# Sixteen of 31 taps of a depthwise convolution as 32x32 diagonal products on the tensor engine

## The chip, the cores and the metric

The kernel runs on one core of a Trainium2 chip, as one program with one launch. The metric is the time of one execution in device microseconds. The engines are TensorE (PE in the profile), VectorE (DVE), ScalarE (ACT), GpSimd (POOL) and SyncE (SP), which issues DMAs.

## The reference, cut to what matters

The program is a small network in float32; the change concerns the convolution inside its "even mixer". That mixer projects 512 latent tokens and 256 context tokens with one matrix. The first columns of the result are gated and go through a depthwise convolution of 31 taps along the tokens, each of the 512 channels with its own 31 weights, and then a layer norm and a SiLU. The rest are queries, keys and values of an attention.

```python
def depthwise_conv(x, w, b=None):
    width = w.shape[0]
    left = (width - 1) // 2
    y = lax.conv_general_dilated(x, w[:, None, :].astype(x.dtype), (1,), [(left, width - 1 - left)],
                                 dimension_numbers=('NWC', 'WIO', 'NWC'), feature_group_count=x.shape[-1])
    return y if b is None else y + b
...
def conformer_conv(p_glu, conv_w, conv_b, ln_g, ln_b):
    a, gate = jnp.split(p_glu, 2, axis=-1)
    u = depthwise_conv(a * jax.nn.sigmoid(gate), conv_w, conv_b)
    return jax.nn.silu(layer_norm(u, ln_g, ln_b))
...
def even_mixer(...):
    p_lat = h_lat @ w_in
    conv_lat = conformer_conv(p_lat[..., :EV_Q0], conv_w, conv_b, ln_g, ln_b)
    q_lat = apply_axial_rope(qk_heads(p_lat[..., EV_Q0:EV_K0]), rope)
    k_lat = apply_axial_rope(qk_heads(p_lat[..., EV_K0:EV_V0]), rope)
    v_lat = v_heads(p_lat[..., EV_V0:])
    ...
```

## The kernel before

Activations lie with features on the 128 partitions and tokens along the free axis. The 512 channels of the convolution are four tiles `conv[0]` to `conv[3]`, and each has two regions of tokens, 512 latent and 256 context columns. A scheduler fixes one static order of instructions for each engine before the run; a loop's generator steps only suggest which work is near which.

Dense products are float32 in three products of two float32r parts. `wsplit` loads a weight piece with a DMA (`wraw`, three buffers), ACT rounds it to `whi` (L73), and VectorE, or GpSimd for four of the tiles, subtracts to get `wlo` (L74), two buffers each. `gemm` then issues L90, L91 and L92 for each of eight row tiles.

The even mixer has three stretches here. In the first part (about 80 to 218 us) the eight gating projections run together with the filter spectra of another layer (the `hy...` names). VectorE forms the gated inputs `us` (whose tile has the name `xl`, L420) and tap 0 of the convolution (L421). In the q/k stage (about 218 to 309) eight tiles of queries and keys are projected, 512 and then 256 columns each. VectorE applies the rotary embedding (L494 to L496) and GpSimd adds its two terms (L497). In the v stage (about 309 to 375) the value projection follows (columns of 256, evacuated by ACT at L511) and the layer norm of the convolution `conv_norm` (its mean's products at L465, its broadcast at L121). Then attention begins (`S`, L571). Between the weight tiles, steps of modulation products are inserted (`mods`, L153): they use the four column strips of the array, 32 output partitions each, and L157 copies their bank on ACT.

The remaining 30 taps are written as a generator, one step per channel tile and region. Taps 29 and 30 are products on ACT and sums on GpSimd (L444, L447, L448, L452); taps 1 to 28 are 28 multiply-adds on VectorE, one after another on the same output (L449 to L451):

```python
for j in range(1, 29):
    nc.vector.scalar_tensor_tensor(out=o, in0=u[:, j:j + n], scalar=cw[:, i, j:j + 1], in1=o,
                                   op0=ALU.mult, op1=ALU.add)
nc.gpsimd.tensor_tensor(out=o, in0=o, in1=o2, op=ALU.add)
```

The scheduler has moved many of the taps forward into the first part, as soon as a tile's inputs exist. PSUM has eight banks of 512 float32 columns. In the even mixer four are the main pool `ps`, two belong to the modulation products (`mps`), and two to the filter spectra in the first part and to the norm (`cps`) afterwards.

`sum4` is a constant of 128 rows by 32 columns, four 32x32 identities above one another. A product with it as the stationary operand adds four groups of 32 partitions.

## Time and profile before

| what | value |
|---|---|
| time, median of 3 runs | 3722.39 us (3717.83 to 3723.65) |
| span of the profiled execution | 3715.1 us |
| TensorE, VectorE busy in the span | 3512.9 us, 2178.3 us |
| ACT, GpSimd busy in the span | 1375.5 us, 740.5 us |
| mean granted TensorE clock | 0.979 of full speed |

The profiled execution is known by its span, from its first instruction to its last; beside it stand the three timed runs, whose median is 7.3 us longer. Busy time of TensorE includes time in which a product runs at a lower clock. A granted clock of 1 is the level of 2.4 GHz.

### The profile page before, as it was taken

How to read it: one execution, taken by the hardware profiler on the slowest of the kernel's cores; microseconds unless marked ns; L12 is line 12 of the kernel's file. 1: busy time of each engine (PE TensorE's matmuls, PEld its weight loads, DVE VectorE, ACT ScalarE, POOL GpSimd, SP SyncE). 2: the span in 40 equal slices, each digit the busy share in tenths (PEclk: the TensorE clock that was granted, in tenths of full speed). 3: DMA queues.
4: the chain of work that ended last, by engine and by line, in shares of the span. 5: the costliest groups of instructions: out<-in, count | busy, mean ns of one | idle time of the engine just before them, and what ended most of it. 6: DMA issues, size and time to landing. Idle time of an engine off the chain costs nothing.

```text
span 3715.1 us, 52350 instructions
## 1 busy us (share of the span) xinstructions
PE 3512.9 (95%) x20932; PEld 2830.7 (76%) x20932; DVE 2178.3 (59%) x3655; ACT 1375.5 (37%) x2393; POOL 740.5 (20%) x637
## 2 busy tenths in 40 slices
PE   6998989999998899989999989999999989999999
PEld 4766778888887667667888877768888877778887
DVE  7998876544458765554333676654334676754333
ACT  4213643222226434233223444542223554642222
POOL 0133201102203333211111032022112132013111
PEclk9998999999999999999999999999999999999999
DMA  5244113333323223332222313233333213243232
GB/s 197 80 159 131 49 50 124 122 119 119 118 102 116 84 75 101 99 130 79 97 92 96 111 55 105 91 127 94 94 96 103 98 52 121 71 133 92 91 96 91
DMA packets 146172, 376.99 MB, mean 101 GB/s; under 512 B 18023, under 2 KB 42983, under 8 KB 145544
## 3 DMA queue, kind: packets, MB, share of 16 engines
q1 hardware_dynamic: 145928, 373.65, 31.0%
q8 instruction: 164, 2.69, 0.3%
q14 instruction: 80, 0.66, 0.1%
HBM read 341.61 MB, written 28.84 MB: 100 GB/s over the span
## 4 chain that ended last, share of the span: by engine, by line
PE 54%; DVE 7%; ACT 3%; issue 2%; POOL 2%; DMA 0%; SPq 0%; DVEq 0%; POOLq 0%; ACTq 0%
PE acc L90 16%; PE acc L92 16%; PE acc L91 16%; DVE wlo L74 1%; DVE hb L1576 1%; PE rec L1301 1%; PE rec L1302 1%; PE rec L1286 1%; ACT whi L73 1%; ACT mp L1811 0%; DVE oz L819 0%; PE acc L1378 0%; PE acc L1377 0%; PE acc L1379 0%; POOL yt L1542 0%
## 5 line engine op out<-in xcount | busy, mean ns | idle before, releaser
L73 ACT CAST whi<-wraw 128x1024 fp32r<-128x1024 f32 (+2 forms) x508 | 493.9, 973 | 1353.4 <-PE acc L91 1014.1
L74 DVE TENSOR_TENSOR wlo<-wraw,whi 128x1024 fp32r<-128x1024 f32 (+2 forms) x504 | 584.2, 1160 | 204.5 <-ACT whi L73 198.0
L90 PE MATMUL acc<-hh,whi 128*128 128x512 f32 (+1 forms) x1024 | 368.2, 360 | 10.9 <-ACT whi L73 7.7
L92 PE MATMUL acc<-hh,wlo 128*128 128x512 f32 (+1 forms) x1024 | 365.3, 358 | 10.2 <-POOL wlo L74 5.6
L91 PE MATMUL acc<-hl,whi 128*128 128x512 f32 (+1 forms) x1024 | 366.5, 358 | 0.7 <-DVE hl L256 0.3
L90 PE MATMUL acc<-fhh,whi 128*128 128x512 f32 x704 | 279.4, 397 | 0.0
L91 PE MATMUL acc<-fhl,whi 128*128 128x512 f32 x704 | 279.1, 396 | 0.0
L92 PE MATMUL acc<-fhh,wlo 128*128 128x512 f32 x704 | 279.1, 396 | 0.0
L91 PE MATMUL acc<-hidl,whi 128*128 128x512 f32 (+1 forms) x768 | 274.4, 357 | 0.9 <-DVE hidl L85 0.9
L90 PE MATMUL acc<-hidh,whi 128*128 128x512 f32 (+1 forms) x768 | 274.6, 358 | 0.0
L92 PE MATMUL acc<-hidh,wlo 128*128 128x512 f32 (+1 forms) x768 | 274.3, 357 | 0.0
L341 POOL TENSOR_TENSOR sqr<-relu 128x512 f32<-128x512 f32 (+1 forms) x96 | 130.6, 1362 | 682.6 <-ACT relu L339 682.6
L90 PEld LDWEIGHTS acc<-hh,whi 128*128 128x128 f32 x1024 | 196.1, 192 | 51.1 <-ACT whi L73 12.5
L92 PEld LDWEIGHTS acc<-hh,wlo 128*128 128x128 f32 x1024 | 195.5, 191 | 43.8 <-DVE wlo L74 7.5
L91 PEld LDWEIGHTS acc<-hl,whi 128*128 128x128 f32 x1024 | 197.2, 193 | 32.8 <-DVE hl L256 2.7
L92 PE MATMUL acc<-shh,wlo 128*128 128x512 f32 (+1 forms) x480 | 194.1, 405 | 8.2 <-DVE wlo L74 8.2
L90 PE MATMUL acc<-shh,whi 128*128 128x512 f32 (+1 forms) x480 | 195.7, 408 | 3.5 <-ACT whi L73 3.5
L91 PE MATMUL acc<-shl,whi 128*128 128x512 f32 (+1 forms) x480 | 194.7, 406 | 0.0
L91 PEld LDWEIGHTS acc<-hidl,whi 128*128 128x128 f32 x768 | 145.3, 189 | 24.5 <-DVE hidl L85 1.3
L90 PEld LDWEIGHTS acc<-hidh,whi 128*128 128x128 f32 x768 | 144.3, 188 | 23.3
L92 PEld LDWEIGHTS acc<-hidh,wlo 128*128 128x128 f32 x768 | 144.3, 188 | 22.9
L92 PEld LDWEIGHTS acc<-fhh,wlo 128*128 128x128 f32 x704 | 132.6, 188 | 32.3
(630 smaller groups left out, 7912.9 us busy)
## 6 DMA issues: line engine op xcount, KB each, us to landing
wraw<-in_mlp_w_dram SPq DMA_DIRECT2D x128, 512.0 KB, 3.2
wraw<-in_ada_w_dram SPq DMA_DIRECT2D x96, 512.0 KB, 3.8
wraw<-in_w_in_dram SPq DMA_DIRECT2D x58, 512.0 KB, 3.3
wraw<-in_w_gate_dram SPq DMA_DIRECT2D x44, 512.0 KB, 3.5
wraw<-in_w_up_dram SPq DMA_DIRECT2D x44, 512.0 KB, 3.5
wraw<-in_od_w_fm_dram SPq DMA_DIRECT2D x36, 512.0 KB, 3.3
wraw<-in_w_down_dram SPq DMA_DIRECT2D x32, 448.0 KB, 3.3
wraw<-in_hy_dft_dram SPq DMA_DIRECT2D x34, 256.0 KB, 2.6
```

Of the source, the lines that this page charges most:

```text
L73: nc.scalar.copy(hi, raw)
L74: (eng or nc.vector).tensor_tensor(out=lo, in0=raw, in1=f32(hi), op=ALU.subtract)
L90: nc.tensor.matmul(out, s[0], m[0], start=first, stop=False)
L91: nc.tensor.matmul(out, s[0], m[1], start=False, stop=False)
L92: nc.tensor.matmul(out, s[1], m[0], start=False, stop=last)
L341: nc.gpsimd.tensor_tensor(out=s, in0=r, in1=r, op=ALU.mult)
L1286: nc.tensor.matmul(vn_ps[pf[d], hd], wT[:, c, pf[d]], S[:, c], start=True, stop=True)
L1301: nc.tensor.matmul(op_[pf[d], hd], qd[:, c, pf[d]], S[:, c], start=True, stop=False)
L1302: nc.tensor.matmul(op_[pf[d], hd], at[pf[d], c], vn[pf[d], hd], start=False, stop=True)
L1576: nc.vector.tensor_tensor_scan(out=b[:, hd], data0=rst, data1=lf[:, hd], initial=0.0, op0=ALU.mult, op1=ALU.add)
```

## The change

Taps 13 to 28, sixteen of them, leave VectorE. For each channel tile and region (a unit) `strips` makes 64 products on TensorE. The stationary operand of one is a 32x32 block with one tap's 32 weights on its diagonal (`dia`, made once by four GpSimd products), and the moving one is 32 channels of the gated input, shifted by the tap. The row strip `q` of the array is the group of 32 channels and chooses one of four PSUM banks; the column strip `s` is one of four taps and chooses 32 output partitions of the bank. Four rounds cover the 16 taps and accumulate. ACT copies the four banks to `e` (tile `cve`). One unit later `joined` adds the four taps' parts with `sum4`, one product per group of channels; ACT copies the result (`cv4`) and VectorE adds it to `conv`.

The PSUM pools change: `ps` has three banks instead of four; the modulation products have two banks only in the block that comes before the first part, and one afterwards; `cps` has four from the q/k stage on.

```diff
+P0, PT = 13, 16
...
-        ps = hp.enter_context(k.pool("evps", 4, space=PSUM))
-        mps = hp.enter_context(k.pool("evmps", 2, space=PSUM))
+        ps = hp.enter_context(k.pool("evps", 3, space=PSUM))
...
-                with k.pool("ada", side="right") as mp:
+                with k.pool("ada", side="right") as mp, k.pool("evmps", 2, space=PSUM) as mps:
...
+        mps = hp.enter_context(k.pool("evmps1", 1, space=PSUM))
+        cps = hp.enter_context(k.pool("evcps", 4, space=PSUM))
...
+            dia = pp.tile([128, 4, PT, 32], F32, name="cdia")
+            for i in range(4):
+                nc.gpsimd.tensor_tensor(out=dia[:, i], in0=k.sum4.unsqueeze(1).to_broadcast([128, PT, 32]),
+                                        in1=cw[:, i, P0:P0 + PT].unsqueeze(2).to_broadcast([128, PT, 32]), op=ALU.mult)
+
+            def strips(i, r):
+                c0, n = regs[r]
+                bank = [k.tmp([128, 512], "acc", pool=cps, bufs=None) for _ in range(4)]
+                for t in range(0, PT, 4):
+                    for s in range(4):
+                        for q in range(4):
+                            p = slice(32 * q, 32 * q + 32)
+                            u0 = c0 + 30 * r + P0 + t + s
+                            nc.tensor.matmul(bank[q][32 * s:32 * s + 32, :n], dia[p, i, t + s], us[p, i, u0:u0 + n], start=t == 0, stop=t + 4 >= PT)
+                e = k.tmp([128, 4, T], "cve", bufs=1, pool=pp)
+                for q in range(4):
+                    nc.scalar.copy(e[:, q, :n], bank[q][:, :n])
+                return i, r, e
+
+            def joined(i, r, e):
+                c0, n = regs[r]
+                acc = k.tmp([128, 512], "acc", pool=ps, bufs=None)[:, :n]
+                for q in range(4):
+                    nc.tensor.matmul(acc[32 * q:32 * q + 32], k.sum4, e[:, q, :n], start=True, stop=True)
+                o3 = k.tmp([128, T], "cv4", bufs=1, pool=pp)[:, :n]
+                nc.scalar.copy(o3, acc)
+                o = conv[i][:, c0:c0 + n]
+                nc.vector.tensor_tensor(out=o, in0=o, in1=o3, op=ALU.add)
...
             def taps():
+                last = None
                 for i in range(4):
                     for r, (c0, n) in enumerate(regs):
+                        new = strips(i, r)
+                        if last:
+                            joined(*last)
+                        last = new
...
-                        for j in range(1, 29):
+                        for j in range(1, P0):
...
+                joined(*last)
                 for r in range(2):
                     yield from conv_norm(r)
...
-            cps = hp.enter_context(k.pool("evcps", 2, space=PSUM))
```

The static order shows where the products stand. In the changed kernel the lines have other numbers: the gemm's three products are L92 to L94, the modulation products L155 and L162, the strips L456, the joining products L467, the mean of the norm L508 and its broadcast L123. Buffer numbers follow the names.

On TensorE, before, the end of one q/k tile (256 columns), a modulation step and the start of the next tile (512 columns):

```order
L92 MATMUL acc_1765<-hh,wlo_1731 128x256
L153 MATMUL acc_1614<-wraw_1825,cs 32x512 x2
L153 MATMUL acc_1614<-wraw_1829,cs 32x512 x2
L90 MATMUL acc_1839<-hh,whi_1835 128x512
L91 MATMUL acc_1839<-hl,whi_1835 128x512
L92 MATMUL acc_1839<-hh,wlo_1836 128x512
```

At the same boundary in the change, the last of a unit's 64 strip products (context region) stands ahead, then the joining products of the unit before it:

```order
L456 MATMUL acc_1860<-xl_505,cdia 32x256
L467 MATMUL acc_1930<-cve_1763,sum_90 32x512 x4
L155 MATMUL acc_1623<-wraw_1956,cs 32x512 x2
L155 MATMUL acc_1623<-wraw_1960,cs 32x512 x2
L92 MATMUL acc_1970<-hh,whi_1966 128x512
L93 MATMUL acc_1970<-hl,whi_1966 128x512
L94 MATMUL acc_1970<-hh,wlo_1967 128x512
```

One whole unit stands between two tiles of the q/k stage, in one piece.

On VectorE, before, in the q/k stage, one tile's rotary embedding and the `wlo` of the next weight, with taps behind it (the two kinds alternate for 16 rows until the next embedding):

```order
L494 STREAM_SHUFFLE rt_364_1760<-acc_1734 128x512
L495 TENSOR_TENSOR rt_363_1759<-acc_1734,c_rope2d 128x512
L496 TENSOR_TENSOR rt_364_1760<-rt_364_1760,c_rope2d 128x512
L74 TENSOR_TENSOR wlo_1836<-wraw_1833,whi_1835 128x1024
L450 SCALAR_TENSOR_TENSOR conv_113<-xl_504,c_ev_conv_w,conv_113 128x256
L450 SCALAR_TENSOR_TENSOR conv_114<-xl_504,c_ev_conv_w,conv_114 128x512
```

At the next tiles of the change, the add of a joined unit (L471) stands where the taps were:

```order
L76 TENSOR_TENSOR wlo_1967<-wraw_1964,whi_1966 128x1024
L471 TENSOR_TENSOR conv_109<-conv_109,cv_377_1935 128x512
L536 STREAM_SHUFFLE rt_387_1996<-acc_1970 128x512
L537 TENSOR_TENSOR rt_386_1995<-acc_1970,c_rope2d 128x512
L538 TENSOR_TENSOR rt_387_1996<-rt_387_1996,c_rope2d 128x512
L76 TENSOR_TENSOR wlo_2137<-wraw_2134,whi_2136 128x1024
L471 TENSOR_TENSOR conv_109<-conv_109,cv_395_2105 128x256
```

From here on VectorE has no tap left in the q/k stage; all remaining ones stand ahead.

On TensorE, before, the mean's products of the norm (L465) stand among the v products:

```order
L92 MATMUL acc_2547<-whi_2475,hl 128x256
L90 MATMUL acc_2547<-whi_2491,hh 128x256
L465 MATMUL acc_2577<-ones,cv_451_2573 128x1 x4
L90 MATMUL acc_2612<-whi_2475,hh 128x256
L91 MATMUL acc_2612<-wlo_2476,hh 128x256
```

In the change they stand close behind the joining products of the last latent unit, with two modulation steps between, and the broadcast (L123) follows at once:

```order
L456 MATMUL acc_2886<-xl_505,cdia 32x256
L467 MATMUL acc_2956<-cve_2781,sum_90 32x512 x4
L155 MATMUL acc_2305<-wraw_2982,cs 32x512 x2
L162 MATMUL acc_2988<-c_ada_sel,wraw_2986 128x4 x4
L508 MATMUL acc_3106<-ones,cv_507_3102 128x1 x4
L123 MATMUL acc_3113<-diag_3114,ones 128x128
```

So the norm's first products now come directly behind the last strips and ahead of most of the v products.

## Rows read from the trace of the kernel before

**Rows 1.** The page's head: the span, then each engine's busy time, share and instructions.
```profile
span 3715.1 us, 52350 instructions
...
PE 3512.9 (95%) x20932; PEld 2830.7 (76%) x20932; DVE 2178.3 (59%) x3655; ACT 1375.5 (37%) x2393; POOL 740.5 (20%) x637
```

**Rows 2.** Windows by stage, one core: length, busy us of each engine, clock, DMA share, GB/s.
```profile
80.00:218.00 138.00, 122.39 (x555) 93.21 (x553) 129.50 (x196) 41.36 (x66) 26.80 (x16) 0.95 0.31 100
218.00:309.00 91.00, 81.96 (x456) 62.74 (x456) 90.72 (x141) 15.54 (x25) 37.80 (x19) 0.98 0.40 138
309.00:375.00 66.00, 53.56 (x377) 45.23 (x377) 48.47 (x80) 24.89 (x43) 21.16 (x15) 0.87 0.49 150
```

**Rows 3.** Waits of TensorE, 80 to 218, eight kinds: us in total, times, longest.
```profile
PE acc L92 <- DVE wlo L74: 5.1, 6, 1.4
...
PE acc L90 <- DVE hyspec L713: 0.2, 1, 0.2
```

**Rows 4.** The same view, 218 to 375.2, nine kinds.
```profile
PE acc L90 <- ACT whi L73: 6.7, 4, 5.3
PE acc L92 <- POOL wlo L74: 5.6, 3, 2.4
PE acc L91 <- DVE wlo L74: 3.4, 2, 2.4
PE acc L92 <- DVE wlo L74: 2.2, 3, 1.0
```

**Rows 5.** Timeline of TensorE, 228 to 239: start, us, line, tiles, shapes.
```profile
228.37 0.50 PE L90 MATMUL acc<-hh,whi 128*128 128x512 f32 x1
...
230.13 0.40 PE L90 MATMUL acc<-hh,whi 128*128 128x512 f32 x1
230.37 0.39 PE L91 MATMUL acc<-hl,whi 128*128 128x512 f32 x1
...
237.25 1.06 PE L153 MATMUL acc<-wraw,cs 128*32 128x512 f32 x8
238.25 0.50 PE L90 MATMUL acc<-hh,whi 128*128 128x512 f32 x1
238.59 0.40 PE L91 MATMUL acc<-hl,whi 128*128 128x512 f32 x1
```

**Rows 6.** Groups of VectorE by line and form, 66 to 400: busy, mean ns.
```profile
L450 DVE SCALAR_TENSOR_TENSOR conv<-xl,c_ev_conv_w,conv 128x512 f32<-128x512 f32 x112 | 96.7, 864 | 0.0
L450 DVE SCALAR_TENSOR_TENSOR conv<-xl,c_ev_conv_w,conv 128x256 f32<-128x256 f32 x112 | 66.9, 597 | 0.1
```

**Rows 7.** Records of line L153, 237.20 to 237.60, then to 238.20: ns min/median/max, first and last start.
```profile
L153 PE MATMUL acc<-wraw,cs x4: 617/617/617, 237.3 to 237.3; 128*32 128x512 f32 x4
...
L153 PE MATMUL acc<-wraw,cs x8: 592/604/617, 237.3 to 237.7; 128*32 128x512 f32 x8
```

**Rows 8.** Timeline of TensorE, 1229.8 to 1231.
```profile
1229.86 0.75 PE L1201 MATMUL prep<-R,LM 32*32 32x32 f32 x64
```

**Rows 9.** Groups of ACT by form, 66 to 400.
```profile
L511 ACT COPY vv<-acc 128x256 f32<-128x256 f32 x12 | 4.4, 369 | 16.0 <-PE acc L92 16.0
...
L157 ACT COPY wraw<-acc 128x512 f32<-128x512 f32 x3 | 1.8, 587 | 2.0 <-PE acc L153 1.7 <-issue 0.4
```

**Rows 10.** Groups of VectorE by form, 66 to 400.
```profile
L471 DVE TENSOR_TENSOR conv<-conv,acc 128x512 f32<-128x512 f32 x4 | 2.7, 680 | 0.0
```

**Rows 11.** Groups of GpSimd by form, 66 to 400.
```profile
L452 POOL TENSOR_TENSOR conv<-conv,cv 128x512 f32<-128x512 f32 x4 | 7.6, 1910 | 36.8 <-DVE conv L450 36.8
```

**Rows 12.** Timeline of all engines, 308 to 322.
```profile
309.76 5.32 DVE L450 SCALAR_TENSOR_TENSOR conv<-xl,c_ev_conv_w,conv 128x512 f32<-128x512 f32 x8
...
311.66 0.83 ACT L554 CAST QS<-b 64x768 fp32r<-64x768 f32 x1 [2.93 <-POOL b L497]
...
314.45 0.58 PE L90 MATMUL acc<-whi,hh 128*128 128x256 f32 x1 [5.34 <-ACT whi L73]
```

**Rows 13.** Windows, 310 to 320.
```profile
310.00:320.00 10.00, 3.15 (x12) 1.20 (x13) 10.00 (x12) 6.66 (x8) 6.78 (x4) 0.56 0.20 61
```

## The prediction

> **What bounds the kernel now.** I read the page first. TensorE is busy for 95% of the span and VectorE for 59% [rows 1], so a change that moves work from VectorE to TensorE must find a stretch in which VectorE, not TensorE, sets the pace. The windows of the even mixer are such a candidate: VectorE is busy 129.5 of 138 us in its first part and 90.7 of 91 us in the q/k stage [rows 2]. But TensorE is not idle there either: 122.4 of 138, 82.0 of 91 and 53.6 of 66 us. What TensorE leaves idle in the three windows is 15.6 + 9.0 + 12.4 = 37 us, and no relief of VectorE can return more than that, apart from the clock.
>
> The waits of TensorE say what the idle time is. Its eight kinds in the first part run from 5.1 us on the `wlo` pieces of VectorE down to 0.2 and add up to 14.7 us [rows 3]. The nine kinds in the q/k and v stages add up to 22.3 us: 6.7 on the ACT cast `whi`, 5.6 on the GpSimd `wlo`, 3.4 + 2.2 on the VectorE `wlo`, and the rest on five others [rows 4]. The timeline shows what a q/k tile costs when nothing is late: 9.88 us from one tile's first product (228.37) to the next one's (238.25), in a stretch without a wait: 24 products of 512 columns at 0.23 to 0.24 us, 24 of 256 at half of that, and the block of modulation products [rows 5]. Eight tiles took 91 us, 11.4 each. So TensorE's own work is 87% of a tile there, and VectorE's fullness costs about 1.5 us a tile.
>
> The longest single wait shows how VectorE's taps reach TensorE [rows 12]. Eight taps stand together from 309.76 for 5.32 us; the rope results that ACT casts to `QS` come late (311.66, after 2.93 us idle for GpSimd's sum), the weight cast `whi` stands behind such casts, and TensorE starts its v product at 314.45 after 5.34 us. In 310 to 320 the granted clock is 0.56, a mean that lies between the levels 1.2 and 2.4 GHz and close to the lower one [rows 13].
>
> **The change, part by part.** *Taken from VectorE:* 128 of the 224 taps, 64 of 512 columns at 864 ns and 64 of 256 at 597 [rows 6]: 55.3 + 38.2 = 93.5 us of VectorE. Eight adds replace them, at most 8 x 0.68 = 5.4 us [rows 10]. VectorE has 269 us of work in 295; after it about 181. It is then not the limit of any of the three windows.
>
> *Added to TensorE:* 512 products of 32 rows by 32 columns, 64 for each of eight units (four channel tiles times a stream of 512 and one of 256 tokens). The trace has no such product with a long moving side. The nearest rows are the modulation products: also float32, 512 columns, on the four column strips. Four of them show eight records, so each product takes two passes: four records start at 237.3 (617 ns each), and four more by 237.7 [rows 7]. The four strips run beside one another, and a pass lasts about 0.45 us (the block of 8 occupies 1.00 us to the next tile's start, which with two passes is at most 0.50; twice a 512-column product's 0.234 is 0.47; the starts lie 0.4 apart). That row strips also run beside one another is shown by 64 records of 32x32 products on diagonal tiles that take 0.75 us together, 12 ns each [rows 8]. So I take all 16 tiles of the array as running together. A unit then has four rounds (16 taps over four column strips) of two passes: 8 x 0.45 = 3.6 us for 512 columns and 1.8 for 256. Entering and leaving such a block costs some 0.3 us (237.25 to 238.25 is 1.00 for two passes of 0.45; the product before it ends its slot 0.09 earlier, and the tile's second product follows at 0.34 instead of 0.23) [rows 5]. Four channel tiles: 4 x (3.9 + 2.1) = 24.0 us. The joining products are four column strips once, two passes, 0.9 and 0.45 us: 4 x 1.35 = 5.4 us. **TensorE gets 29.4 us more.** None of it is hidden: TensorE runs its queue in order, and its only empty slots are the waits counted below.
>
> The lower end, with passes of 0.40 us, is 26.6 us. The upper ends come from how far the 16 tiles hold one another up, and are the rivals below.
>
> The Trainium skill (TensorE: Matmul & The Clock Gate, Part 3, "The mechanism") says that matmuls start and end strictly in program order. Taken literally, a product's second pass waits for its own first pass, and everything behind it too; [rows 7], with four first passes at 237.3 and the second ones at 237.7, speak against so strict a reading. By that rule the sum would be the last rival's.
>
> *Given back, q/k and v stages.* Of the 22.3 us of waits, those on the `whi` casts (6.7) and on the VectorE `wlo` pieces (5.6) stand behind taps and should go: **-12.3**. The GpSimd `wlo` (5.6) stays: GpSimd keeps its sums and gets four products of 128x512 (about 4 x 1.9 = 7.6 us by its nearest row) [rows 11]. The 4.4 us of others stay.
>
> *Given back, first part.* In VectorE's order, 55 taps of 512 and 37 of 256 columns stand ahead of the first part's last evacuation before, and 42 and 36 after. That is 13 x 0.864 + 0.6 = 11.8 us less. TensorE waits 14.7 us there, mostly for VectorE's pieces. A share of one half, **-6**, lies between nothing (the weights are late for other reasons, and the main PSUM pool drops from four banks to three) and the whole 11.8.
>
> *Given back, clock.* The window 309 to 375 runs at 0.87 [rows 2], which costs it (1 - 0.87) x 66 = 8.6 us against full speed. Denser work there may hold the clock: I take half, **-4**.
>
> *Hidden.* ACT makes 32 + 8 copies of banks: 20 x 0.587 + 20 x 0.369 = 19.1 us [rows 9]; it is busy 40 of 157 us in the last two windows, and a unit's copies (2.3 us) have a whole tile of about 14 us until its four banks are wanted again. If that cover is gone, each is on TensorE's way with 2.3 us. The modulation products lose one of two banks; their copy and transposition (0.6 us, three times) are small.
>
> *New waits.* In TensorE's order the norm's products (L508) stand right behind the joining products of the last unit of 512 columns, with two steps of modulation between. Joining leads to them by an ACT copy (0.59), the add into `conv` (0.68) and the last add of the mean's sum (0.68 by the same row): 1.9 us in which TensorE has one modulation block, and behind it stand the norm's broadcast and the `v` products, which attention waits for. I put **+2**, since the broadcast's own small steps follow as well. The four copies of the unit ahead (2.3 us) lie beside the unit of 256 columns (2.1) that TensorE runs in between.
>
> *Sum.* 29.4 - 12.3 - 6 - 4 + 2 = +9.1 us on the profiled 3715.1. The median of the three runs, 3722.4, is 7.3 above the span, so 3722.4 + 9.1 = 3731.5: **3732 us**. A change within 0.2% (7.4 us) can hardly be told from none; the forecast stands just above that edge.
>
> **The rivals.**
> 1. *Forecast,* the 16 tiles together with the returns as put down: 3732, own range 3717 to 3742. Chance 0.43.
> 2. *VectorE is the true pace of the first part and the q/k stage (faster).* Then every us taken from it ahead of the last evacuation returns (11.8), all waits of the later stages go (22.3), and the clock comes back in full (8.6): 29.4 - 42.7 = -13.3, 3709 (the 2 us at the norm are then covered too). For it: 99.7% busy in 218 to 309. Against it: 9.88 of 11.4 us of a tile are TensorE's own. It decides for faster once more than 37 us come back. Chance 0.20.
> 3. *New waits take the recovery's place.* The chain at the norm lies bare from the four copies on (2.3 + 0.9 + 1.9 with the same again for the broadcast, some 7 in place of 2) and three banks cancel the first part's 6: +20, 3742. Against it: VectorE empties banks sooner. Chance 0.18.
> 4. *Second passes block a strip.* The four products of one tap can run together, but the next tap's wait for a pass: 16 slots of 0.45 us a unit, 7.2 and 3.6, so 4 x 11.4 (with edges) + 5.4 = 51; the returns stay at 22.3 and the norm's 2: +31, 3753. Chance 0.12.
> 5. *Only four tiles ever run together:* 16 rounds of two passes, 14.4 and 7.2: 4 x 22.2 + 5.4 = 94, net +74, 3796. Chance 0.05.
> 6. *Each product waits for its own first pass:* 64 x 0.45 = 28.8 us for a unit of 512, 14.4 for one of 256: 4 x 43.8 + 5.4 = 181, net +160, 3883. The strict order of the Trainium skill's page would give this. Chance 0.02.
>
> **How the numbers follow.** The range runs from 3708 (the faster rival) to 3756 (the fourth); about 0.07 lies above, some 0.1 below. Faster than 3715: 0.15 of rival 2, 0.03 of the forecast's spread: 0.18. Within 0.2%: 0.05 of rival 2, 0.17 of the forecast, 0.04 of rival 3: 0.26. Slower than 3730: the rest, 0.56.
>
> **What would show it.** In the rows of the diagonal products (L456, 1,024 records): a block of 3.6 to 3.9 us for a unit of 512 says 16 tiles together; 7, 14 or 29 us says rival 4, 5 or 6. A q/k tile's period of about 14 us (9.9 + 3.9 or 2.1 + joining) without waits on `whi` and the VectorE `wlo` says that the returns came as put down; less than 12 would speak for rival 2. VectorE's share should fall to about 60% in both later windows. A wait of TensorE at the norm's products (L508) behind the copies of the last unit would be rival 3, and waits for PSUM banks in the first part too. I would be wrong most if products of different row strips that write to the same partitions of four banks held one another up, of which the trace before has no row, or if the first part's waits are not VectorE's doing.

## The result and the profile after

The change made the kernel slower: 3746.07 us median of 4 runs (3737.38 to 3748.94) against 3720.59 us of the kernel before, timed beside it (4 runs, 3717.83 to 3723.65). The ratio is 1.0072, with a 95% interval of 1.0055 to 1.0089. The forecast of 3732 us had the direction; the time lies inside the range of 3708 to 3756, and the loss, 25.5 us, is nearly three times the 9.1 that the sum gave.

The head of the page of the changed kernel, which answers to [rows 1]:

```profile
span 3742.8 us, 54487 instructions
...
PE 3545.7 (95%) x22020; PEld 2848.4 (76%) x22020; DVE 2104.9 (56%) x3535; ACT 1391.7 (37%) x2433; POOL 731.5 (20%) x641
```

The span is 27.7 us longer. TensorE is busy 32.8 us more and VectorE 73.4 us less.

The windows of the changed kernel, first over the stretches of [rows 2]; busy time in the order TensorE, weight load, VectorE, ACT, GpSimd, then the clock:

```profile
80.00:218.00 138.00, 120.84 (x577) 93.99 (x575) 126.59 (x181) 43.55 (x70) 35.57 (x26) 0.97 0.33 103
218.00:309.00 91.00, 90.70 (x1180) 64.82 (x1180) 37.65 (x56) 21.89 (x43) 22.29 (x15) 0.98 0.36 120
309.00:375.00 66.00, 59.78 (x598) 43.96 (x596) 27.35 (x44) 23.64 (x41) 18.71 (x11) 0.90 0.45 138
...
80.00:226.60 146.60, 129.14 (x616) 100.94 (x615) 135.19 (x194) 44.60 (x71) 40.36 (x29) 0.97 0.34 110
226.60:323.00 96.40, 96.40 (x1331) 67.36 (x1330) 32.76 (x48) 23.55 (x48) 20.90 (x13) 1.00 0.31 100
323.00:397.00 74.00, 64.86 (x552) 50.54 (x550) 29.95 (x55) 28.79 (x53) 18.86 (x13) 0.91 0.47 143
```

VectorE falls from 90.7 to 37.7 of 91 us in the q/k stretch, and TensorE rises from 82.0 to 90.7. In the first part VectorE is still busy 126.6 of 138 us: hardly anything left it there. The last three rows are the same view with other cuts: since the stages have moved, I cut each trace at the start of the first and of the last rotary product (the VectorE product that reads a q/k tile's bank and the rope table), and at the first attention score. The kernel before has 149.0, 78.9 and 67.2 us between these cuts. So the first part is 2.4 us shorter, the q/k stage 17.5 us longer, the v stage 6.8 us longer. Of the 2.4 us, 2.1 were there before any tap: the first gating product starts at 61.2 us instead of 63.3, behind the same order of TensorE and VectorE. The first score starts at 397.0 instead of 375.1, 21.9 us later. The other 5.8 us of the span are lost after the mixer, in stretches whose work the change does not touch. Those stretches differ between all the profiles here: from the first score to the end they took 3339 to 3355 us, and the time of low clock in them differs with them. I read nothing from these 5.8 us.

The strips in the changed kernel, two boundaries of q/k tiles in the timeline of TensorE (the unit of 512 columns, then one of 256 with the joining products of the first):

```profile
227.36 4.47 PE L456 MATMUL acc<-xl,cdia 32*32 32x512 f32 x128
231.76 1.06 PE L155 MATMUL acc<-wraw,cs 128*32 128x512 f32 x8
...
241.27 2.76 PE L456 MATMUL acc<-xl,cdia 32*32 32x256 f32 x128
243.96 1.06 PE L467 MATMUL acc<-cve,sum 128*32 128x512 f32 x8
244.85 1.04 PE L155 MATMUL acc<-wraw,cs 128*32 128x512 f32 x8
```

From a unit's start to the next work are 4.40 us (227.36 to 231.76) and 2.69 us (241.27 to 243.96); the joining products take 0.89 us. So the 16 tiles do run together; rivals 4 to 6, with 7, 14 or 29 us, are out. How a unit of 512 comes to 4.40 instead of 3.9 stands in the records of its first 1.4 us (three windows one behind another, 227.30 to 227.55, to 228.40, to 228.75; each lists every record that overlaps it, so a record can stand in two; first and last start):

```profile
L456 PEld LDWEIGHTS acc<-xl,cdia x32: 101/103/105, 227.4 to 227.5; 32*32 32x32 f32 x32
L456 PE MATMUL acc<-xl,cdia x16: 612/612/612, 227.4 to 227.5; 32*32 32x512 f32 x16
...
L456 PE MATMUL acc<-xl,cdia x33: 586/589/612, 227.4 to 228.2; 32*32 32x512 f32 x33
L456 PEld LDWEIGHTS acc<-xl,cdia x11: 101/104/105, 227.4 to 228.2; 32*32 32x32 f32 x11
...
L456 PE MATMUL acc<-xl,cdia x32: 586/589/610, 227.8 to 228.7; 32*32 32x512 f32 x32
L456 PEld LDWEIGHTS acc<-xl,cdia x31: 101/102/105, 228.4 to 228.7; 32*32 32x32 f32 x31
```

In the first window all 32 weight loads of the first round and 16 first passes start. By the middle window 16 second passes have followed (0.45 us after the first ones, without a gap) and one product of the next round. Then the weight loads stand in line: 31 of them come from 228.4 on, together with the products of the second round. By the starts of the records the second round begins 1.08 us after the first, where two passes are 0.90. Four rounds of 1.08 make 4.3 of the 4.40 us, and in the unit of 256 four of 0.65 make 2.6 of the 2.69. So a step of 0.18 us from round to round separates these units from the 3.6 and 1.8 us of the forecast, not the edge of 0.3 that I added.

The waits of TensorE from the first rotary product to the first score (answering to [rows 4]):

```profile
PE acc L123 <- DVE diag L122: 2.7, 3, 1.7
PE acc L92 <- ACT whi L75: 1.6, 2, 1.2
PE acc L162 <- ACT wraw L159: 1.5, 1, 1.5
PE acc L93 <- DVE wlo L76: 1.2, 1, 1.2
...
PE acc L508 <- DVE cv L505: 0.9, 1, 0.9
```

In the q/k stage TensorE has no wait at all any more (96.40 of 96.40 us busy). The kernel before has 5.8 us on `whi`, 5.6 on GpSimd's `wlo` and 5.1 on VectorE's between these cuts; 1.6, nothing and 1.2 are left. Waits at the norm's broadcast (L123), its mean (L508) and the modulation (L162) have come in their place in the v stage.

On SP the reload of `x` (L365) now stands ahead of the first value weight:

```profile
311.16 0.33 SPq L152 DMA_DIRECT2D wraw<-in_ada_w_dram  x1
327.89 1.52 SPq L365 DMA_DIRECT2D xl<-in_x_dram  x2
329.46 0.44 SPq L72 DMA_DIRECT2D wraw<-in_ev_w_v_dram  x1
```

The two rows of L365 could start only when the last strip had read the tile that `x` goes into (16.4 us of waiting in the chain of SP's waits), and the value weight stood behind them until 329.46. In the kernel before the first value weight was issued at 296.97. I had not looked at SP's order.

### The profile page after: what moved, and what is told of

Same layout as the page of the kernel before. It is cut to its first block, busy times and chain, and to the rows that moved or that the text cites. A ratio compares the mean times of both kernels' runs of the same rounds, so it can differ in the third digit from the quotient of the medians.

```text
span 3742.8 us, 54487 instructions
## 1 busy us (share of the span) xinstructions
PE 3545.7 (95%) x22020; PEld 2848.4 (76%) x22020; DVE 2104.9 (56%) x3535; ACT 1391.7 (37%) x2433; POOL 731.5 (20%) x641
## 4 chain that ended last, share of the span: by engine, by line
PE 54%; DVE 7%; ACT 3%; issue 2%; POOL 2%; DVEq 0%; POOLq 0%; ACTq 0%
PE acc L92 16%; PE acc L94 16%; PE acc L93 16%; DVE wlo L76 1%; DVE hb L1618 1%; PE rec L1343 1%; PE rec L1344 1%; PE rec L1328 1%; ACT whi L75 0%; ACT mp L1853 0%; PE acc L1420 0%; PE acc L1419 0%; DVE oz L861 0%; PE acc L1421 0%; PE rec L1337 0%
## 5 line engine op out<-in xcount | busy, mean ns | idle before, releaser
L92 PE MATMUL acc<-hh,whi 128*128 128x512 f32 (+1 forms) x1024 | 365.8, 357 | 11.8 <-ACT whi L75 8.6
L94 PE MATMUL acc<-hh,wlo 128*128 128x512 f32 (+1 forms) x1024 | 364.0, 356 | 8.3 <-DVE wlo L76 8.3
L92 PE MATMUL acc<-fhh,whi 128*128 128x512 f32 x704 | 279.4, 397 | 0.0
L94 PE MATMUL acc<-fhh,wlo 128*128 128x512 f32 x704 | 279.1, 396 | 0.0
L92 PE MATMUL acc<-hidh,whi 128*128 128x512 f32 (+1 forms) x768 | 274.9, 358 | 0.0
L94 PE MATMUL acc<-hidh,wlo 128*128 128x512 f32 (+1 forms) x768 | 274.6, 358 | 0.0
L92 PEld LDWEIGHTS acc<-hh,whi 128*128 128x128 f32 x1024 | 194.5, 190 | 51.0 <-ACT whi L75 11.8
L94 PEld LDWEIGHTS acc<-hh,wlo 128*128 128x128 f32 x1024 | 194.2, 190 | 41.3 <-DVE wlo L76 11.0
L94 PE MATMUL acc<-shh,wlo 128*128 128x512 f32 (+1 forms) x480 | 193.7, 404 | 7.8 <-DVE wlo L76 7.8
L92 PE MATMUL acc<-shh,whi 128*128 128x512 f32 (+1 forms) x480 | 196.1, 408 | 3.5 <-ACT whi L75 3.5
L92 PEld LDWEIGHTS acc<-hidh,whi 128*128 128x128 f32 x768 | 145.1, 189 | 23.3
L94 PEld LDWEIGHTS acc<-hidh,wlo 128*128 128x128 f32 x768 | 145.1, 189 | 23.0
L94 PEld LDWEIGHTS acc<-fhh,wlo 128*128 128x128 f32 x704 | 132.6, 188 | 32.3
```

The lines of the kernel that those rows point to most:

```text
L92: nc.tensor.matmul(out, s[0], m[0], start=first, stop=False)
L94: nc.tensor.matmul(out, s[1], m[0], start=False, stop=last)
```

## The experiments

Twelve kernels, each timed in five rounds beside the kernel before (3716 to 3720 us in these sessions). They were built on the changed kernel unless said otherwise. The order of the text is that of the argument. Ratios are to the kernel before, with 95% intervals.

| kernel | us | ratio | first part, q/k, v (us) | first score at |
|---|---|---|---|---|
| before | 3720.6 | 1 | 149.0, 78.9, 67.2 | 375.1 |
| the change | 3746.1 | 1.0072 [1.0055, 1.0089] | 146.6, 96.4, 74.0 | 397.0 |
| 1 reload late | 3744.9 | 1.0078 [1.0066, 1.0090] | 151.9, 95.9, 69.9 | 397.7 |
| 2 and all taps | 3781.5 | 1.0173 [1.0160, 1.0186] | 150.8, 135.3, 72.2 | 438.3 |
| 3 no strips | 3720.0 | 1.0009 [1.0000, 1.0019] | 150.6, 73.3, 68.7 | 372.6 |
| 4 eight taps | 3738.3 | 1.0061 [1.0049, 1.0073] | 148.8, 93.4, 68.6 | 390.8 |
| 5 no taps | 3698.4 | 0.9947 [0.9935, 0.9959] | 140.3, 69.5, 65.2 | 355.0 |
| 6 pools only | 3724.6 | 1.0022 [1.0014, 1.0031] | 146.9, 84.0, 69.4 | 380.3 |
| 7 one pass | 3733.6 | 1.0042 [1.0030, 1.0054] | 150.4, 79.4, 68.5 | 378.3 |
| 8 column inner | 3745.8 | 1.0074 [1.0061, 1.0087] | 151.9, 96.0, 74.8 | 402.7 |
| 9 held, no strips | 3721.5 | 1.0006 [0.9998, 1.0015] | 137.0, 93.1, 67.2 | 377.3 |
| 10 held, strips | 3755.1 | 1.0101 [1.0085, 1.0116] | 136.9, 124.5, 72.0 | 413.4 |
| 11 held, one pass | 3750.8 | 1.0087 [1.0073, 1.0101] | 138.4, 108.6, 72.2 | 399.2 |
| 12 relief, old pools | 3706.2 | 0.9973 [0.9963, 0.9983] | 142.8, 68.1, 68.0 | 358.9 |

**1, the reload held back.** One VectorE element is read from the gated inputs together with the normalized convolution, so the reload has to come after the norm; in SP's order the value weights then stand ahead of it. All other runs but 6 contain this edit too.

```diff
                 for r in range(2):
                     yield from conv_norm(r)
+                    if r == 0:
+                        z = k.tmp([128, 1], "usz", bufs=1, pool=tp_)
+                        nc.vector.tensor_tensor(out=z, in0=us[:, 3, 0:1], in1=conv[3][:, 0:1], op=ALU.add)
```

> The change, with the reload of x held back until after the norm of the latent region, so that in SP's order the four value weights stand ahead of it. Theory A (the v stage lost time because the first value weights were queued on SP behind the reload, which waited 16.4 us for the last strips): the first value product comes directly behind the strips, the v stage is about 8 us shorter, 3738 us (3733 to 3742). Rival B (the stage is long because the norm's products and broadcast stand ahead of the v products on TensorE, and the weights would be on time anyway): no change, 3743 to 3749.

Its order moved as meant, the first value weight left SP 6.5 us before the last rotary product began (321.35, 327.8) instead of after it, and the first value evacuation came 25.5 us after that product instead of 32.1. The time did not move: 1.0078 against 1.0072. Theory A falls as an account of the lost time. The v stage's 4.1 us less can't be credited to it either, since run 8, the same kernel but for an inner loop, has 74.8 us there; the mean granted clock of that stage is 0.97 in the one and 0.91 in the other (run 1, then run 8):

```profile
327.80:397.70 69.90, 61.18 (x550) 49.23 (x550) 29.50 (x56) 28.81 (x52) 18.54 (x13) 0.97 0.50 144
...
327.90:402.70 74.80, 65.75 (x552) 51.60 (x550) 29.54 (x56) 28.95 (x52) 18.50 (x13) 0.91 0.45 134
```

The first part of this run is 5.3 us longer than that of the change though the orders of TensorE and VectorE are the same there. The mean granted clock is 0.94 in it against 0.97, but run 8, with the same order once more, took 151.9 us at 0.97 too. So the clock is not the whole of it, and what the rest is stays open.

**3, no strips: the relief without its price.** The calls of `strips` and `joined` are left out, so sixteen taps are missing.

```diff
-                        new = strips(i, r)
-                        if last:
-                            joined(*last)
-                        last = new
...
-                joined(*last)
```

> As the first run, but the strips and the joining products are left out, and VectorE makes 12 taps: sixteen taps are missing from the result; the relief without its price. Theory A: the price is 34 us, so 34 us below the first run, about 3704, that is 16 to 17 us below the kernel before. The faster rival of the prediction (VectorE sets the pace, 42.7 us come back): about 3678.

Both expectations failed: 3720.0 us, no faster than the kernel before, with 93 us less on VectorE. The difference to run 1 is the strips' net price, 24.9 us, of which the q/k stage holds 22.6 (95.9 against 73.3). But that VectorE's relief alone was worth nothing had to have a reason.

**12, the same relief with the old pools.** The kernel before, where taps 13 to 28 are left out.

```diff
-                        for j in range(1, 29):
+                        for j in range(1, 13):
```

> The kernel before with its own PSUM pools, where taps 13 to 28 are simply left out (sixteen taps are missing) and the reload of x is held back: the relief of VectorE without strips, joining, diagonals and the change's pools. Theory A3 (the relief falls on the q/k stage, where TensorE is near its own floor, and little of it leaves the first part): at most 8 us faster than the kernel before, 3711 to 3720 beside its 3716 to 3720. Rival (the relief is worth more, and in the run without strips the change's pools ate it): 3708 or less beside 3716, 10 to 16 us below the run without strips.

The rival was right: 3706.2 us, 0.9973. The same relief gives 10 us with the pools of the kernel before, and nothing with the change's pools and diagonals. Its windows with the stage cuts:

```profile
80.00:222.80 142.80, 126.46 (x589) 98.19 (x591) 133.30 (x194) 43.14 (x70) 34.58 (x25) 0.96 0.35 113
222.80:290.90 68.10, 66.92 (x380) 51.41 (x373) 25.70 (x41) 10.13 (x15) 19.95 (x12) 1.00 0.43 147
290.90:358.90 68.00, 58.02 (x405) 48.35 (x405) 33.60 (x53) 25.42 (x44) 18.61 (x13) 0.90 0.51 151
```

Against [rows 2]'s kernel the first part gives 6.2 us and the q/k stage 10.8; the v stage gives nothing. TensorE is busy 66.9 of 68.1 us in the q/k stage, so that stage is near its floor.

Not all of the 6.2 us is the relief. In TensorE's and VectorE's order the two kernels are the same up to 104 us, taps included, and run 12 is 3.2 us ahead from the first gating product on (it starts at 60.0 us; in the other profiles at 61.2 to 63.4). Executions differ by that much there, so the relief gave the first part about 3 us. The first score comes 16.2 us earlier; without the 3.2 that is 13, of which the medians show 10.

The same view of run 3:

```profile
80.00:230.60 150.60, 131.44 (x626) 103.06 (x628) 135.83 (x193) 44.65 (x72) 40.28 (x29) 0.97 0.32 107
230.60:303.90 73.30, 69.18 (x379) 53.29 (x372) 25.70 (x43) 9.35 (x14) 21.77 (x13) 0.95 0.40 137
303.90:372.60 68.70, 60.41 (x408) 48.54 (x406) 33.04 (x50) 25.17 (x43) 18.59 (x13) 0.90 0.49 141
```

It loses 7.8 us in the first part and 5.2 in the q/k stage against run 12, with the same taps left to VectorE. Of the 7.8 us, 1.4 were there at the first gating product, up to which the orders are the same. In the q/k stage TensorE has a single wait of 3.2 us on VectorE's `wlo`, and the clock is 0.95 instead of 1.00.

**6, the pools alone,** on the kernel before, with its 28 taps and no edit of the reload.

```diff
-        ps = hp.enter_context(k.pool("evps", 4, space=PSUM))
-        mps = hp.enter_context(k.pool("evmps", 2, space=PSUM))
+        ps = hp.enter_context(k.pool("evps", 3, space=PSUM))
...
+        mps = hp.enter_context(k.pool("evmps1", 1, space=PSUM))
+        cps = hp.enter_context(k.pool("evcps", 4, space=PSUM))
```

> The kernel before with only the PSUM pools of the change (three banks for the main pool, one for the modulation products, four for the norm), 28 taps on VectorE. Theory A2: the pools cost nothing, 3713 to 3721 beside a kernel before of 3716. Rival (part of the change's loss is the lost bank, the prediction's third case): 5 us or more above the kernel before. Its trace also gives a second look at how far the first part and the time behind the mixer move between executions.

The rival was right again: 3724.6 us against 3716.1, 1.0022 [1.0014, 1.0031]. The pools of the change cost something by themselves. Part of how can be seen. The scheduler makes another order from them, and the mean of the norm now stands in TensorE's order where VectorE is not done with its taps. The waits of TensorE in its v stage:

```profile
PE acc L466 <- DVE cv L463: 11.9, 1, 11.9
PE acc L153 <- DMA wraw<-in_ada_w_dram: 1.9, 3, 0.8
PE acc L121 <- DVE diag L120: 1.8, 3, 0.7
```

11.9 us in one wait for VectorE's sum; the kernel before had 0.5 there. In the changed kernel VectorE is free by then and the same place costs 0.9 (L508). What the pools cost there lies in the first part and the q/k stage, as runs 3 and 12 show.

One piece of it stands ahead of 80 us, where the stage cuts begin: right behind the first two gating products TensorE's order differs for the first time. The kernel before, then run 6:

```profile
63.88 0.63 PE L91 MATMUL acc<-hl,whi 128*128 128x512 f32 x1
64.30 0.63 PE L90 MATMUL acc<-hh,whi 128*128 128x512 f32 x1
64.73 0.63 PE L91 MATMUL acc<-hl,whi 128*128 128x512 f32 x1
65.16 0.63 PE L92 MATMUL acc<-hh,wlo 128*128 128x512 f32 x1
...
63.97 0.63 PE L91 MATMUL acc<-hl,whi 128*128 128x512 f32 x1
68.56 0.80 PE L92 MATMUL acc<-hh,wlo 128*128 128x512 f32 x1 [3.96 <-DVE wlo L74]
```

VectorE forms two `wlo` pieces at the same places in both kernels (from 63.4 and 67.2 us; from 63.5 and 67.3). Before, TensorE has two parts of one product behind it and goes on, by these times, with another, whose `wlo` is the piece that is already there. In run 6 it stays with the first product and stands still for 3.96 us until the second piece is done. This wait of 4.0 us is in the change and in every run but 12; the kernel before and run 12, with four main banks, do not have it. In run 6 the delay is nearly made up by the last gated input (187.0 us against 186.1), in run 3 it is not (188.4 against 179.7 in run 12). The rest I could not split into the lost bank itself, the other two pools, the order that follows from them, and the four GpSimd products of the diagonals (5.7 us).

**2, the price without the relief.** VectorE makes all 28 taps beside the strips (sixteen are added twice).

```diff
-                        for j in range(1, P0):
+                        for j in range(1, 29):
```

> As the run before, but VectorE makes all 28 of its taps again beside the strips, so sixteen taps are added twice: the price of the strips without the relief. Theory A (TensorE sets the pace, and VectorE's full load only costs what its lateness costs): some 34 us are added to TensorE and the longer stage leaves VectorE enough room, so it comes out 0 to 8 us above the run before, about 3743. Rival (VectorE's load is what counts, as in the faster rival of the prediction): the whole 34 us on the time of before, 3755 or more, 15 to 20 us above the run before.

3781.5 us, even above the rival. It is no clean price: a profile of VectorE shows up to 41 taps (34 and 7) in one row between two rotary products, 26 us, where a q/k tile with its unit takes some 14; the q/k tiles come 25 to 29 us apart at first. TensorE waits in that stage:

```profile
PE acc L456 <- ACT cve L459: 21.7, 2, 12.1
PE acc L155 <- DVE mods L163: 3.8, 1, 3.8
```

A unit's banks are not copied in time. Why the scheduler set so many taps there I did not look into. So the run shows only that the relief matters once the strips are there.

**4, eight taps on TensorE.**

```diff
-P0, PT = 13, 16
+P0, PT = 21, 8
```

> As the first run with 8 taps on TensorE instead of 16 (two rounds a unit), 20 on VectorE. Theory A, by the rounds of 1.075 and 0.65 us in the trace: 4 units of each kind save two rounds, 4 x 2 x (1.075 + 0.65) = 13.8 us; VectorE stays below full. 12 to 14 us below the first run, about 3725. Rival (a unit costs by its start and end and its copies, not by its rounds): less than 6 us below the first run.

6.6 us below run 1, half of the expectation. The units shrank as expected, to 2.28 us (230.65 to 232.93) and 1.43 (242.56 to 243.99), with the same step of 1.08 from round to round. The rest is in VectorE: 24 taps, twelve of 512 and twelve of 256 columns, stand in one stretch of 12.78 us in the second q/k tile, and TensorE waits 5.5 us in a stage in which run 1 has none.

**7, one pass a product.** The diagonals in bfloat16, the moving side the upper half of each float32 number, so that sixteen taps are rounded.

```diff
-            dia = pp.tile([128, 4, PT, 32], F32, name="cdia")
+            dia = pp.tile([128, 4, PT, 32], mybir.dt.bfloat16, name="cdia")
...
-... us[p, i, u0:u0 + n], start=t == 0, ...
+... us[p, i, u0:u0 + n].bitcast(mybir.dt.bfloat16)[:, 1:2 * n:2], start=t == 0, ...
```

> As the first run, with the strips in bfloat16 (the moving side is the upper half of each float32 number, so the sixteen taps are rounded): each product is one pass at a column a cycle instead of two slower ones. If a unit costs its passes and the step from round to round (theory A), a unit of 512 falls from 4.4 to about 1.1 to 1.6 us and one of 256 from 2.7 to about 0.7 to 1.2: 17 to 20 us less on TensorE, 3725 to 3728. Rival (the loss is not the passes but the copies, the joining and the changed order): less than 8 us below the first run.

A unit of 512 takes 1.10 us, 64 records in one train:

```profile
230.13 1.17 PE L456 MATMUL acc<-xl,cdia 32*32 32x512 bf16 x64
231.23 0.64 PE L155 MATMUL acc<-wraw,cs 128*32 128x512 f32 x4
```

The first score starts at 378.3, 19.4 us before run 1, as Theory A had it; of the time only 11.2 us arrived (3733.6), between the two expectations. In its profile a later stage of the program that no edit touches (from the first 32x32 product named `prep` to the last 128x128 one, `prep<-R,kg`) took 337.8 us against 326.0 in run 1, at a mean granted clock of 0.94 against 0.98, so a good part of the difference is there; why it fell so is open. Four rounds one after another, each 0.23 us, have no step between them: in these runs the 0.18 us appear only with two passes, thus two weight loads, a product. The run changes the type along with the passes, so it does not show which of these makes the step.

**8, the other order of the inner loops.**

```diff
-                    for s in range(4):
-                        for q in range(4):
+                    for q in range(4):
+                        for s in range(4):
```

> As the first run, with the four column strips (taps) in the inner loop and the row strips outside: the same products in another order. Theory A (between two rounds the 16 tiles wait because weight loads go in line, and the line stands at the first tile's second load): the round stays at 1.07 us and the time within 3 us of the first run. Rival (products that follow one another into the same column strip and four banks hold each other up): a round of 0.9 us, 5 us less.

3745.8 us, as run 1, and the rounds again begin 1.08 us apart. So the rival is out: which strips follow one another makes no difference here. That the weight loads in line are the reason, as Theory A has it, is not shown by this.

**5, no taps on VectorE** (run 3, with the 12 remaining taps left out too).

```diff
-                        for j in range(1, P0):
+                        for j in range(1, 1):
```

> As the run without strips, and VectorE's remaining 12 taps a unit are left out as well (28 taps are missing from the result): VectorE has some 70 us less again, most of them in the first part. Theory A2 (the first part's waits are the chain of weight load, cast and subtraction, which taps hardly lengthen, and the v stage hangs on its own weights and the norm): the time stays within 8 us of the run without strips, 3712 to 3722. Rival (VectorE's taps set the pace of the first part, as the prediction's returned 6 us supposed): the first part falls by 10 us or more, 3705 or less.

The rival was right: 21.5 us below run 3, 3698.4. The first part falls from 150.6 to 140.3 us, and TensorE's waits on `wlo` of VectorE in it from 7.1 to 0.5. The two lines (run 3, then run 5, each in its first part):

```profile
PE acc L94 <- DVE wlo L76: 7.1, 6, 2.7
...
PE acc L94 <- DVE wlo L76: 0.5, 1, 0.5
```

So VectorE's taps do hold the first part up. In run 3 it had lost little there: of the 96 taps that the change leaves, 88 with 64.5 us stand before 229 us, where the kernel before had 71.0. In run 12 all 96 stand there, with 66.8 us.

**9 to 11, the remaining taps held back.** Each unit's 12 taps use weights that are formed after that unit's q/k tile is rotated, so none can stand in the first part; without strips, with strips, and with strips in bfloat16 (rounded).

```diff
+                        cw2 = k.tmp([128, 31], "cw2", bufs=2, pool=tp_)
+                        nc.vector.scalar_tensor_tensor(out=cw2, in0=qk[2 * i + r][:, 0:31], scalar=0.0, in1=cw[:, i],
+                                                       op0=ALU.mult, op1=ALU.add)
                         for j in range(1, P0):
...
-... scalar=cw[:, i, j:j + 1], in1=o,
+... scalar=cw2[:, j:j + 1], in1=o,
```

> As the run without strips (sixteen taps missing), but VectorE's 12 remaining taps of each unit are held back until that unit's q/k tile has been rotated: none of them stands in the first part any more, and the amount of work is the same. Theory A3 (relief is worth something only where it leaves the first part: there VectorE's order puts taps ahead of the pieces that TensorE waits for, while in the q/k stage TensorE is at its own floor): the first part falls by 7 to 10 us as in the run without any taps, and the whole to 3708 to 3714. Rival (it is the amount of taps, wherever they stand): no better than the run without strips, 3716 to 3722.

> The whole computation: the first run (strips, joining, 16 taps on TensorE) with the 12 taps held back in the same way. Theory A3: 7 to 10 us below the first run, 3735 to 3738, still above the kernel before, since the strips' price of about 25 us stays. Rival (held taps come out of the norm's start or of the q/k stage instead): 3742 or more.

> The run before with the strips in bfloat16 (sixteen taps rounded). Theory A3: the two effects add up, 16 to 20 us below the first run's 3745, 3722 to 3728, so that even with one pass a product the change only comes near the kernel before. Rival (they hide one another): as the one-pass run, 3733.

Half of A3 came true, and the half that mattered did not. Runs 9 (3721.5) and 10 (3755.1) came out as their rivals said, and run 11 (3750.8) above both of its expectations. The first part fell to 137.0, 136.9 and 138.4 us, 13.6 us below run 3 in run 9. The q/k stage took it back and more: 93.1 us against 73.3 in run 9, 124.5 against 95.9 in run 10. The windows of run 9:

```profile
80.00:217.00 137.00, 128.31 (x614) 102.33 (x613) 74.23 (x105) 38.75 (x62) 23.98 (x16) 0.96 0.36 117
217.00:310.10 93.10, 79.11 (x424) 60.36 (x423) 83.86 (x121) 16.91 (x27) 34.93 (x23) 0.93 0.34 114
310.10:377.30 67.20, 52.47 (x376) 45.67 (x377) 43.23 (x69) 24.73 (x41) 22.00 (x15) 0.85 0.46 140
```

VectorE is at 83.9 of 93.1 us in the q/k stage. TensorE waits 12.4 us there, 5.1 on GpSimd's `wlo`, 3.1 on VectorE's, 3.0 on `whi` and 1.2 on a modulation copy, where run 3 had 4.1. That the taps now stand in the way there is likely, but no single wait shows it. The hold itself adds a wait (for GpSimd's sum of the rotated tile), so the size is not that of the taps alone.

## Why the prediction came out as it did

In the runs the loss splits into three pieces, each the difference of two kernels, against a kernel before of 3716 us: the relief, -10 us (run 12); the pools with the diagonals, +13 (run 12 to run 3, 0.9973 to 1.0009); the strips with copies and joining, +25 (run 3 to run 1). The sum is +28; run 1 measured +29, the change +26.8 by its ratio.

Beside the forecast's terms: the strips with the wait at the norm were put at +31.4 and cost 25; the returns were put at -22.3 and gave 10; the pools and diagonals were put at nothing and cost 13. So the sum was missed twice by about as much, by 12 in the returns and by 13 in the pools, and the 6 us that the strips cost less hid a part. The direction is no luck, since 25 is more than 10 even without the pools. That 3746 lies inside the range is luck in part: the forecast's own case ended at 3742, and the room above that, up to 3756, was there for rival 4, which the trace excludes.

*TensorE's added work,* forecast 29.4 us: in the trace 4 x (4.40 + 2.69) = 28.4 for the units and 6.8 busy for the joining products, some 35. The mechanism (16 tiles together, two passes of 0.45 us) was right. The term was mis-sized by the step from round to round, 0.18 us, which I had no row for, and in whose place I had put one edge of 0.3 us a unit. The net price in time is 25 us, since the strips also fill what would be waits: in the q/k stage TensorE is busy 69.2 of 73.3 us at a clock of 0.95 without them (run 3), and all of 95.9 us at 1.00 with them (run 1). The lower end of this term, with passes of 0.40 us, adds up to 26.4 and not to 26.6; nothing hangs on it. Rivals 4 to 6 are excluded by the unit's 4.40 us.

*The strict order* that the Trainium skill states (TensorE: Matmul & The Clock Gate, Part 3, "The mechanism") would have made the last rival. The trace does not agree with that reading: 16 first passes start within 0.10 us, before any second one. What it does show in line are the weight loads of the later rounds.

*Returned in the q/k and v stages,* forecast 12.3 us: near in size in run 12 (10.8 and -0.8), wrong in place, since the v stage gave nothing in any run with 12 taps; its waits were replaced by others. And 4.4 us of the waits that went in the q/k stage were those on GpSimd's `wlo` (5.6 to 1.2), which the forecast had left standing.

*Returned in the first part,* forecast 6 us: 6.2 in run 12 and 2.4 in the change, but 3.2 and 2.1 of these were there before the orders part, so about 3 and nearly nothing are left. The term was too large, and the reason I gave for half was not the whole one. VectorE's taps hold that part up (run 5), but the taps that leave are the late ones, and the first twelve of each unit stay in the first part.

*Returned clock,* forecast 4 us in the v stage: not seen; 0.87 became 0.91, and between runs 1 and 8, alike but for an inner loop, it changes by as much.

*The pools* are the step that failed beside the returns. I put the lost bank at nothing, as the lower end of the first part's return, and the smaller modulation pool too, and priced three banks only as part of rival 3. Run 6 shows 8 us for the pools on the kernel before, and runs 3 and 12 show 13 for pools and diagonals under the change. Without these 13 the measured pieces make +15 (25 - 10), 6 above the sum of 9.1. Rival 3, at 3742, came nearest: three banks were one of its two causes. Its sign, waits for PSUM banks in the first part, did not appear; what appeared is another order, with a wait of 4.0 us for a weight piece. The second cause, the norm's chain, costs 0.9 us at L508 and 2.7 at L123, of which the kernel before had 1.0, about the 2 us of the sum.

*Rival 2,* VectorE as the true pace: it was true of the first part in so far as its taps hold that up, and of the q/k stage only down to a floor of 68 to 70 us, which it keeps whatever VectorE has left (runs 5 and 12); the change's strips then lie on top of that floor.

*SP's queue,* which I had not followed: the reload of `x` did hold the value weights for 16.4 us, and cost nothing that run 1 could measure.

*The signs named beforehand:* the period of a q/k tile (12.7 to 14.4 us, without the waits on `whi` and VectorE's `wlo`) came as the returns asked, and yet the sum was short by some 17 us: those signs look at the q/k stage and do not see what another order costs elsewhere. VectorE's share in the two later windows fell to 41%, not 60%, because most taps that are left stand in the first part.

No kernel with the whole computation beat the kernel before. Of those with strips that compute it, the best is run 4 with eight taps, 1.0061.

## What to carry to other kernels

A unit that is full is not yet the unit that sets the pace: take its work away in one run, without paying for it elsewhere, before building the replacement (here 93 us less on VectorE were worth 10). Ask which instructions of the full engine leave, and from which stage; a loop shortened at its end leaves its first steps where they were. Resources that the replacement takes, such as PSUM banks, are a term of their own, because a scheduler makes another order from them; test them alone, and do not expect a lost bank to show as a wait for a bank.

## What the runs showed of the hardware

Sixteen float32 products of 32x32 run together on the array, their passes starting 7 ns apart (16 within 0.10 us) and following on the same tile after 0.45 us for 512 columns; the next round on the same tiles starts 0.18 us late. In the first round all 32 weight loads are done in 0.13 us; in the second 31 of them take 0.26 us, between the passes. With one pass a product (bfloat16, 0.23 us a round) there is no such step. Kernels with the same order in a stage differed there by 5 us: in the v stage of runs 1 and 8, which differ in an inner loop of the strips, with the granted clock (0.97 and 0.91), and in the first part of the change and of run 8 (146.6 and 151.9 us) at the same mean clock of 0.97. That is as much as some of the terms that a forecast adds up.
